# Three small moves in a four-layer fp32 backbone: the reciprocal root, differential attention's reciprocals, and the Nyquist copies

## The chip, the cores and the metric

The kernel runs on one core of a Trainium2 chip. The core has a matrix engine (TensorE; PE in the profile, and PEld for its weight loads), VectorE (DVE), ScalarE (ACT), GpSimd (POOL), SyncE (SP) and DMA queues. Each engine takes its own instructions in its own order, and engines wait for one another through semaphores. The metric is the device time of one launch in microseconds (us), less being better; a comparison uses the median of several launches. Durations of single instructions come from one profiled launch.

## What is computed

A backbone over 512 latent and 256 context tokens of width 1024, four layers deep. Layer i mixes tokens by kind i mod 3 (Fourier, differential attention, latent attention, Fourier again) and then runs a squared-ReLU MLP. Every sub-layer begins with an RMS norm, so a reciprocal root of a mean square stands at the head of each; differential attention has one more norm per head on its output. Cut to what the change touches:

```python
def rms_norm(x, g, eps=RMS_EPS):
    y = x * lax.rsqrt(jnp.mean(x * x, axis=-1, keepdims=True) + eps)
    return y * g

def diff_attend(q1, q2, k1, k2, v, lam):          # 8 heads, two maps each
    p = jax.nn.softmax(s1, axis=-1) - lam * jax.nn.softmax(s2, axis=-1)
    return jnp.einsum("bhqk,bkhe->bqhe", p, v)    # then rms_norm over the head

def fourier_mixer(h, w, bias):                    # layers 0 and 3
    f = jnp.fft.fft2(h_grouped, axes=(1, 3), norm="ortho").real
    return f.reshape(b, s, d) @ w + bias
```

## The kernel before

Activations lie transposed, features on the 128 partitions: `x` is eight tiles of 128 x 768 (512 latent, 256 context columns). Every fp32 matrix product is made of three TensorE products: each operand is split into a high part (a cast on ScalarE, L96) and a low part (a subtraction on VectorE, L97), and high*high, high*low and low*high are summed. So weights, activations and probabilities all pass once through ScalarE and once through VectorE before TensorE can use them. VectorE also adds each layer's result to `x` (`accum`, L375), which is what empties the PSUM buffers that TensorE fills (`pw`, `pu`, `ps` in the rows).

TensorE's program is in the order in which the code is written. The instructions of the other engines are put in order by a scheduler, from priorities and its own cost estimates, so that an edit can move instructions that it does not name. What each place of the change does:

- **`rstd_from`** (L283 to L289) makes `r = 1/sqrt(ms/n + eps)` from a sum of squares `ms` in PSUM: logarithm (L284) and exponential (L286) on ScalarE give a first value, then one Newton step sharpens it: a square on ScalarE (L287), and on VectorE `v` from `ms` (L285), a product (L288) and a fused multiply-add (L289). It is called by the norm that ends an MLP and feeds the next layer (`MixNorm.finish`, L309), by the norm that feeds an MLP (`MlpNorm.stat`, L359), by the head norm of differential attention (`PVb`, L992), by latent attention's two inner norms (`lat_norm`, L1123) and at the start for six columns of one element per partition (L627).
- **`S`** in `diff` (L933 to L959) computes two score maps for a block of 128 query tokens. For each map VectorE takes the row maximum (L952), ScalarE the exponential with its row sum (L953), VectorE the reciprocal of the sum (L954). The second reciprocal is multiplied by lambda on VectorE (L956), ScalarE scales map 2 with it (L957) and VectorE scales map 1 and subtracts (L958). There are 32 such blocks of 768 keys and 16 of 256 keys (context), hence 48 pairs of maps. `Tr` transposes the result on TensorE (L801), `PVa` multiplies by the values, `PVb` normalises. Between these steps TensorE is given work of other heads (`F(...)`): projections, and for the odd heads the output projection `gen_wo`, whose results go to `x` by L375 with two `pw` buffers.
- **`fourier_lat`** (L752, layer 3) transforms along the group's features first: for each of 4 groups and 4 token tiles one product of 258 columns in `pw` (three buffers), split into `fa` (high on ScalarE, low on VectorE, both read `pw`). Column 256, the Nyquist term, is copied from both parts into small tiles `nqh` and `nql` by GpSimd (L777, L778), 32 copies of 128 x 1; a product over the four token tiles (L785) reads them. The first eight products use the first 256 tokens; after the fourth, `flush()` (L781) runs the rest of the previous norm for tokens 256 to 511: a product `ms`, `rstd_from`, and then for each of 8 feature tiles `nu` (VectorE, L328), `hhi` (ScalarE, L329) and `hlo` (VectorE, L330), which the second eight products need. `csl` (L97) are low parts of the table for the second transform.

## Time and profile before

| | |
|---|---|
| time of three launches | 2876.17, 2877.42 (median), 2878.32 us |
| the profiled launch itself | 2874.33 us, of which 2872.5 us are the profile's span |
| mean granted TensorE clock | 0.984 of full |
| instructions | 39661 |
| DMA | 294.00 MB, mean 102 GB/s |

How to read a row of the profile: in a timeline, start and length in us, engine, line, operation, output <- inputs, shapes, count, and in brackets how long the engine sat idle just before and on which instruction it then stopped waiting. In a table of windows: the stretch and its length, busy time (and count) of PE, PEld, DVE, ACT and POOL, the granted TensorE clock as a share of full, the share of DMA time, and GB/s. In the table of waits: the engine and its instruction <- what it waited for, total us, times, longest. In a table by form: line, engine, operation, names, shapes and count | busy us, mean ns | idle time before, with what ended it.

### The profile page before, as it was taken

The numbers are of one execution on the slowest core, as the hardware profiler recorded it, in microseconds if no ns is written. First come the engines' busy times: TensorE is split into PE (matmuls) and PEld (weight loads), VectorE is DVE, ScalarE is ACT, GpSimd is POOL, SyncE is SP. The second block draws the span as 40 slices with busy tenths as digits, with TensorE's granted clock in tenths as the row PEclk, the third lists the DMA queues.
The fourth block names the chain that finished last, engine by engine and source line by source line (L and its number), as shares of the span: only waits on it lengthen the run. The fifth ranks groups of instructions, "written<-read, shape, count | busy, mean of one in ns | idle before, by whom it ended". The sixth has DMA issues, their size and how long they took to land.

```text
span 2872.5 us, 39661 instructions
## 1 busy us (share of the span) xinstructions
PE 2737.2 (95%) x15387; PEld 2357.4 (82%) x15387; DVE 1924.1 (67%) x3371; ACT 1265.6 (44%) x2301; POOL 314.5 (11%) x267
## 2 busy tenths in 40 slices
PE   8999999999999899799999998899899998999998
PEld 5788888888888778688888897788778888888887
DVE  8986665658787778775545448998875546564344
ACT  4542222225575656432323236777543335443332
POOL 0010000002110010100000012665200003100001
PEclk9999999999999999999999999999999998999999
DMA  9454333322111111253333311110455542233231
GB/s 323 149 183 131 111 110 110 110 96 90 44 46 46 40 45 41 96 161 117 112 116 117 96 38 50 33 46 19 149 189 182 165 136 67 92 96 100 77 116 46
DMA packets 95452, 294.00 MB, mean 102 GB/s; under 512 B 11264, under 2 KB 15520, under 8 KB 94752
## 3 DMA queue, kind: packets, MB, share of 16 engines
q1 hardware_dynamic: 92704, 288.33, 31.8%
q0 software_dynamic: 2560, 3.15, 0.6%
q8 instruction: 121, 1.98, 0.3%
q14 instruction: 67, 0.55, 0.1%
HBM read 283.29 MB, written 2.11 MB: 99 GB/s over the span
## 4 chain that ended last, share of the span: by engine, by line
PE 78%; DVE 14%; ACT 4%; DMA 2%; issue 2%; POOL 0%; SPq 0%; POOLq 0%; ACTq 0%; DVEq 0%
PE pw L140 70%; PE pu L140 4%; PE ps L140 3%; DVE ptl L97 2%; DVE x L375 1%; DVE mx L952 1%; PE pu L801 1%; ACT e L1292 1%; DVE mx L1290 1%; DVE wlo L97 1%; DVE nu L328 1%; DVE hlo L330 1%; PE pn L140 1%; DVE hlo L348 0%; DMA raw<-in_w 0%
## 5 line engine op out<-in xcount | busy, mean ns | idle before, releaser
L96 ACT CAST whi<-raw 128x1024 fp32r<-128x1024 f32 (+1 forms) x322 | 308.4, 984 | 1081.4 <-PE pw L140 1018.0
L140 PE MATMUL pw<-hhi,whi 128*128 128x512 f32 (+2 forms) x1680 | 590.3, 351 | 4.1 <-DVE r L450 3.2
L140 PE MATMUL pw<-hlo,whi 128*128 128x512 f32 (+2 forms) x1680 | 589.5, 351 | 0.0
L140 PE MATMUL pw<-hhi,wlo 128*128 128x512 f32 (+2 forms) x1680 | 587.6, 350 | 0.8 <-DVE wlo L97 0.8
L140 PE MATMUL pw<-ahi,whi 128*128 128x512 f32 (+1 forms) x1664 | 568.9, 342 | 1.2 <-ACT ahi L96 1.2
L140 PE MATMUL pw<-alo,whi 128*128 128x512 f32 (+1 forms) x1664 | 567.5, 341 | 1.1 <-DVE alo L97 1.1
L140 PE MATMUL pw<-ahi,wlo 128*128 128x512 f32 (+1 forms) x1664 | 566.3, 340 | 0.0
L375 DVE SCALAR_TENSOR_TENSOR x<-pw,mod,x 128x512 f32<-128x512 f32 (+1 forms) x504 | 302.0, 623 | 286.0 <-PE pw L140 283.2
L97 DVE TENSOR_TENSOR wlo<-raw,whi 128x1024 fp32r<-128x1024 f32 (+1 forms) x322 | 362.5, 1142 | 169.7 <-ACT whi L96 168.4
L140 PEld LDWEIGHTS pw<-hhi,whi 128*128 128x128 f32 x1680 | 318.5, 190 | 48.6 <-issue 3.4
L140 PEld LDWEIGHTS pw<-hhi,wlo 128*128 128x128 f32 x1680 | 318.9, 190 | 44.1 <-DVE wlo L97 1.3
L140 PEld LDWEIGHTS pw<-hlo,whi 128*128 128x128 f32 x1680 | 318.5, 190 | 42.5
L140 PEld LDWEIGHTS pw<-ahi,whi 128*128 128x128 f32 x1664 | 315.6, 190 | 38.5 <-ACT ahi L96 1.7
L140 PEld LDWEIGHTS pw<-alo,whi 128*128 128x128 f32 x1664 | 315.5, 190 | 37.0 <-DVE alo L97 1.6
L140 PEld LDWEIGHTS pw<-ahi,wlo 128*128 128x128 f32 x1664 | 315.2, 189 | 36.2
L264 DVE SCALAR_TENSOR_TENSOR raw<-raw,cb 128x1024 f32<-128x1024 f32 x176 | 214.9, 1222 | 118.6 <-DMA raw<-in_modw 116.9
L307 POOL TENSOR_TENSOR nacc<-nacc,nsq 128x256 f32<-128x256 f32 x70 | 53.2, 760 | 1752.1 <-ACT nsq L306 1751.2
L264 DVE SCALAR_TENSOR_TENSOR junk<-raw,cb 128x1024 bf16<-128x1024 f32 x96 | 118.8, 1238 | 66.4 <-DMA raw<-in_modw 64.6
L1294 POOL TENSOR_SCALAR e<-e,li 128x768 f32<-128x768 f32 x64 | 145.5, 2279 | 93.3 <-DVE li L1293 70.9
L97 DVE TENSOR_TENSOR alo<-r,ahi 128x768 fp32r<-128x768 f32 (+2 forms) x134 | 105.7, 792 | 73.5 <-ACT ahi L96 73.2
L97 DVE TENSOR_TENSOR ptl<-pu,pth 128x384 fp32r<-128x384 f32 (+1 forms) x208 | 106.1, 539 | 8.4 <-ACT pth L96 5.6
L140 PE MATMUL pw<-hhi,g 128*128 128x512 f32 (+2 forms) x384 | 100.9, 344 | 5.0 <-DVE x L375 2.9
(330 smaller groups left out, 4287.1 us busy)
## 6 DMA issues: line engine op xcount, KB each, us to landing
raw<-in_w SPq DMA_DIRECT2D x252, 512.0 KB, 4.0
raw<-in_modw SPq DMA_DIRECT2D x176, 512.0 KB, 3.8
wm<-in_msh SPq DMA_DIRECT2D x32, 256.0 KB, 5.9
raw<-in_fw SPq DMA_DIRECT2D x10, 512.0 KB, 4.0
cb<-scr SPq DMA_DIRECT2D x4, 1024.0 KB, 5.5
raw<-in_dwk SPq DMA_DIRECT2D x16, 256.0 KB, 2.7
raw<-in_dwq SPq DMA_DIRECT2D x16, 256.0 KB, 2.8
raw<-in_dwv SPq DMA_DIRECT2D x16, 256.0 KB, 2.6
```

The lines of the kernel that those rows point to most:

```text
L96: nc.scalar.copy(hi, src)
L97: nc.vector.tensor_sub(lo, src, rd(hi))
L140: r = nc.tensor.matmul(o, lhsT, rhs, start=start, stop=stop)
L264: nc.vector.scalar_tensor_tensor(o, m, 1.0, cb[:, v * 1024:(v + 1) * 1024], op0=ALU.mult, op1=ALU.mult, accum_out=mcol(mod[l, ch], v, k))
L307: nc.gpsimd.tensor_tensor(nacc[:, c0:c0 + w], nacc[:, c0:c0 + w], s, op=ALU.add)
L328: nc.vector.scalar_tensor_tensor(u, xs, am, r, op0=ALU.mult, op1=ALU.mult)
L330: nc.vector.scalar_tensor_tensor(lo, u, sh, rd(hi), op0=ALU.add, op1=ALU.subtract)
L375: nc.vector.scalar_tensor_tensor(xs, src, mcol(mod[l, ch], 0 if c0 < SL else 1, n), xs, op0=ALU.mult, op1=ALU.add)
L801: nc.tensor.transpose(t[:, i * 128:(i + 1) * 128], p[:, (k0 + i) * 128:(k0 + i + 1) * 128], ident)
L952: nc.vector.reduce_max(mx, sv, axis=AX.X, negate=True)
L1290: nc.vector.reduce_max(mx, s[:, :T], axis=AX.X, negate=True)
L1294: nc.gpsimd.tensor_scalar(et, et, li, None, op0=ALU.mult)
```

## The change

`rstd_from` loses one VectorE operation and its scratch tile `v`. The factor one half and 1/n go into the scale of ScalarE's square, and the sum of squares is added to eps*n and multiplied in one VectorE operation that reads PSUM; the last one computes (1.5 - t)*r. In differential attention both row sums go to the two columns of one tile, one reciprocal of 128 x 2 serves both maps, and lambda is applied by a 128 x 1 operation on ScalarE. In layer 3 the Nyquist copies are made by ScalarE in place of GpSimd.

```diff
-    def rstd_from(ms, inv_n, r, t, v):
+    def rstd_from(ms, inv_n, r, t):
         nc.scalar.activation(t, ms, AF.Ln, bias=epst[0:t.shape[0]], scale=inv_n)
-        nc.vector.tensor_scalar(v, ms, -0.5 * inv_n, -0.5 * EPS, op0=ALU.mult, op1=ALU.add)
         nc.scalar.activation(r, t, AF.Exp, scale=-0.5)
-        nc.scalar.activation(t, r, AF.Square)
-        nc.vector.tensor_mul(t, t, v)
-        nc.vector.scalar_tensor_tensor(r, t, 1.5, r, op0=ALU.add, op1=ALU.mult)
+        nc.scalar.activation(t, r, AF.Square, scale=math.sqrt(0.5 * inv_n))
+        nc.vector.scalar_tensor_tensor(t, ms, EPS / inv_n, t, op0=ALU.add, op1=ALU.mult)
+        nc.vector.scalar_tensor_tensor(r, t, 1.5, r, op0=ALU.subtract, op1=ALU.mult, reverse0=True)
...
-                        nc.gpsimd.tensor_copy(nq[t][0][:, 32 * g:32 * g + 1], rd(ah[:, 256:257]))
-                        nc.gpsimd.tensor_copy(nq[t][1][:, 32 * g:32 * g + 1], rd(al[:, 256:257]))
+                        nc.scalar.copy(nq[t][0][:, 32 * g:32 * g + 1], rd(ah[:, 256:257]))
+                        nc.scalar.copy(nq[t][1][:, 32 * g:32 * g + 1], rd(al[:, 256:257]))
...
                 for _, _, o0, w_, e in rows:
-                    ri = []
+                    li = sp.tile([128, 2], F32, name="li", tag="li", bufs=4)
                     for m in range(2):
                         mx = sp.tile([128, 1], F32, name="mx", tag="mx", bufs=4)
-                        li = sp.tile([128, 1], F32, name="li", tag="li", bufs=4)
                         sv = s[m][:, o0:o0 + w_]
                         nc.vector.reduce_max(mx, sv, axis=AX.X, negate=True)
-                        nc.scalar.activation(e[m], sv, AF.Exp, bias=mx, accum_out=li)
-                        nc.vector.reciprocal(li, li)
-                        ri.append(li)
-                    nc.vector.tensor_mul(ri[1], ri[1], lam)
-                    nc.scalar.activation(e[1], e[1], AF.Copy, scale=ri[1])
-                    nc.vector.scalar_tensor_tensor(e[0], e[0], ri[0], e[1], op0=ALU.mult, op1=ALU.subtract)
+                        nc.scalar.activation(e[m], sv, AF.Exp, bias=mx, accum_out=li[:, m:m + 1])
+                    nc.vector.reciprocal(li, li)
+                    nc.scalar.activation(li[:, 1:2], li[:, 1:2], AF.Copy, scale=lam)
+                    nc.scalar.activation(e[1], e[1], AF.Copy, scale=li[:, 1:2])
+                    nc.vector.scalar_tensor_tensor(e[0], e[0], li[:, 0:1], e[1], op0=ALU.mult, op1=ALU.subtract)
```

The callers drop their last argument. The order of TensorE and SyncE is the same in both programs; the scheduler moves instructions on VectorE and ScalarE; three places are shown. Line numbers behind `rstd_from`'s first lines are smaller in the changed program (its L287 and L288 are the two VectorE operations, L776 and L777 the copies, L535 is L536 of before).

VectorE in layer 3 around the flushed norm, before: the fourth low part (`fa_22701`), table parts, the norm's chain, then the fifth low part (`fa_22780`).

```order
L97 TENSOR_TENSOR csl1_22758<-raw_22755,csh1_22757 128x516
L288 TENSOR_TENSOR nt_22709<-nt_22709,nv_22710 128x256
L97 TENSOR_TENSOR csl2_22764<-raw_22761,csh2_22763 128x516
L289 SCALAR_TENSOR_TENSOR nr_22708<-nt_22709,nr_22708 128x256
L97 TENSOR_TENSOR csl3_22770<-raw_22767,csh3_22769 128x516
L328 SCALAR_TENSOR_TENSOR nu_22717<-x0_70,am3_1_119,nr_22708 128x256
L328 SCALAR_TENSOR_TENSOR nu_22721<-x1_71,am3_1_119,nr_22708 128x256
L97 TENSOR_TENSOR fa_22780<-pw_22773,fa_22780 128x258
```

The same place of VectorE in the changed program; `fa_22592`, `fa_22604` and `fa_22616` are the fifth, sixth and seventh low part.

```order
L97 TENSOR_TENSOR csl3_22582<-raw_22579,csh3_22581 128x516
L287 SCALAR_TENSOR_TENSOR nt_22523<-pn_22520,nt_22523 128x256
L97 TENSOR_TENSOR fa_22592<-pw_22585,fa_22592 128x258
L288 SCALAR_TENSOR_TENSOR nr_22522<-nt_22523,nr_22522 128x256
L97 TENSOR_TENSOR fa_22604<-pw_22597,fa_22604 128x258
L327 SCALAR_TENSOR_TENSOR nu_22529<-x0_70,am3_1_119,nr_22522 128x256
L327 SCALAR_TENSOR_TENSOR nu_22533<-x1_71,am3_1_119,nr_22522 128x256
L97 TENSOR_TENSOR fa_22616<-pw_22609,fa_22616 128x258
```

All table parts now stand ahead of the chain, and the fifth and sixth low parts have moved from behind `nu` to between the chain's steps.

ScalarE at the end of the first transform in layer 3, in the changed program: the last two casts, the last four copies, a weight cast `g` and the biases added to `x` (before, the same casts and biases stand there without copies).

```order
L96 CAST fa<-pw 128x258 x2
L776 CAST nqh_22464<-fa 128x1
L96 CAST g<-raw 128x512
L776 CAST nqh_22468<-fa 128x1
L535 ACTIVATE x_70<-x_70,gb 128x512
L777 CAST nql_22465<-fa 128x1
L535 ACTIVATE x_71<-x_71,gb 128x512
L777 CAST nql_22469<-fa 128x1
```

The last copy stands behind one weight cast and two bias operations.

VectorE in differential attention at a head's first output projection, before: head norm, row maxima, the additions to `x`.

```order
L285 TENSOR_SCALAR nv<-pu 128x256
L288 TENSOR_TENSOR nt<-nt,nv 128x256
L289 SCALAR_TENSOR_TENSOR nr<-nt,nr 128x256
L997 SCALAR_TENSOR_TENSOR nu<-nu,gs,nr 128x256
L952 TENSOR_REDUCE mx<-ps 128x1
L375 SCALAR_TENSOR_TENSOR x_71<-pw,mod_2_104,x_71 128x512
L97 TENSOR_TENSOR ol<-nu,oh 128x256
L952 TENSOR_REDUCE mx<-ps 128x1
```

The same place in the changed program (its L994, L950 and L374 are L997, L952 and L375 of before).

```order
L287 SCALAR_TENSOR_TENSOR nt<-pu,nt 128x256
L288 SCALAR_TENSOR_TENSOR nr<-nt,nr 128x256
L994 SCALAR_TENSOR_TENSOR nu<-nu,gs,nr 128x256
L97 TENSOR_TENSOR ol<-nu,oh 128x256
L950 TENSOR_REDUCE mx<-ps 128x1
L374 SCALAR_TENSOR_TENSOR x_71<-pw,mod_2_104,x_71 128x512
L950 TENSOR_REDUCE mx<-ps 128x1
```

`v` is gone, and `ol`, which waits for ScalarE's cast `oh` of `nu`, has moved ahead of the first row maximum and of the first addition to `x`.

More of the change, by code (lines that the diff above doesn't have):

```diff
@@ L314, in finish @@
             r = nt_("r")
-            rstd_from(ms, 1.0 / D, r, nt_("t"), nt_("v"))
+            rstd_from(ms, 1.0 / D, r, nt_("t"))
             v = 0 if c0 < SL else 1
@@ L366, in stat @@
             for c0, ms in zip(range(0, self.T, 256), ps):
-                rstd_from(ms, 1.0 / D, r_all[:, c0:c0 + 256], nt_("t"), nt_("v"))
+                rstd_from(ms, 1.0 / D, r_all[:, c0:c0 + 256], nt_("t"))
     def parts(T):
@@ L626, in fourier_first @@
                     nc.scalar.activation(jk, xr, AF.Square, accum_out=ss[:, 0:1])
-                rstd_from(ss[:, 0:1], 1.0 / D, ss[:, 1:2], ss[:, 2:3], ss[:, 3:4])
+                rstd_from(ss[:, 0:1], 1.0 / D, ss[:, 1:2], ss[:, 2:3])
                 uh = up.tile([128, 1024], F32R, name="uh")
@@ L995, in PVb @@
                 r = nt_("r")
-                rstd_from(ms, 1.0 / 128, r, nt_("t"), nt_("v"))
+                rstd_from(ms, 1.0 / 128, r, nt_("t"))
                 nc.vector.scalar_tensor_tensor(u, u, gs, r, op0=ALU.mult, op1=ALU.mult)
@@ L1127, in lat_norm @@
                 r = qt_("r")[:, :w]
-                rstd_from(ms, inv_n, r, qt_("t")[:, :w], qt_("v")[:, :w])
+                rstd_from(ms, inv_n, r, qt_("t")[:, :w])
                 for i, p in enumerate(ps):
```

## The prediction

> **What bounds the kernel now.** I read the page's busy shares, then the windows, to find the stages in which TensorE waits, and there its waits.
>
> ```profile
> PE 2737.2 (95%) x15387; PEld 2357.4 (82%) x15387; DVE 1924.1 (67%) x3371; ACT 1265.6 (44%) x2301; POOL 314.5 (11%) x267
> core 0: us, PE busy (x) PEld busy (x) DVE busy (x) ACT busy (x) POOL busy (x), PEclk, DMA share, GB/s
> 200.00:250.00 50.00, 50.00 (x289) 44.02 (x288) 37.68 (x59) 15.65 (x20) 0.00 (x0) 1.00 0.44 135
> 760.00:1150.00 390.00, 355.84 (x2290) 315.24 (x2289) 313.11 (x666) 242.94 (x546) 30.66 (x37) 0.99 0.16 42
> 2408.00:2441.00 33.00, 25.43 (x134) 22.51 (x133) 27.10 (x61) 22.28 (x52) 15.75 (x45) 0.74 0.22 67
> ```
>
> TensorE is busy 95% of the span, and in an MLP (200 to 250) without a gap: a reciprocal root that is a little sooner there buys nothing. It is idle 390 - 356 = 34 us in differential attention (760 to 1150), where VectorE is 80% busy, and 7.6 us at the start of layer 3 (2408 to 2441), where its clock is only 0.74 besides. The change touches the work that stands in the way in both. In attention half of that idle time ends on one VectorE operation, the addition to `x` (the table of TensorE's waits):
>
> ```profile
> PE pw L140 <- DVE x L375: 16.7, 16, 2.2
> ```
>
> **Differential attention, step by step.** The operations that go, by form between 700 and 1200, and a pair of rows that shows what a small one really takes:
>
> ```profile
> L954 DVE RECIPROCAL li<-li 128x1 f32<-128x1 f32 x96 | 14.6, 156 | 7.1 <-ACT e L953 4.7 <-ACT nacc L953 1.7
> L285 DVE TENSOR_SCALAR nv<-pu 128x256 f32<-128x256 f32 x25 | 10.5, 421 | 15.7 <-ACT nt L284 15.5
> L956 DVE TENSOR_TENSOR li<-li,lam 128x1 f32<-128x1 f32 x48 | 7.3, 152 | 0.5
> 993.59 0.15 DVE L956 TENSOR_TENSOR li<-li,lam 128x1 f32<-128x1 f32 x1
> 993.66 0.68 DVE L874 TENSOR_TENSOR qt<-qt,qsw 128x512 f32<-128x512 f32 x1
> ```
>
> 48 reciprocals and 48 products go, and 25 computations of `v`. By busy time that is 7.3 + 7.3 + 10.5 = 25.1 us. But a small operation lets the next one start 0.07 us after itself, so the 96 small ones may free only 6.7 us, and 25 of `v` at 0.42 free 10.5: 17 us at the low end, 25 at the high end, of 313 us. I take 17, for the next operation's start is what counts on a busy VectorE.
>
> Little of it will reach TensorE. Of the 15.7 us that VectorE stood before `v`, none is won by its going: the product behind it waits for ScalarE's square, two operations later, and its successor waits there in the same way. The rows at one output projection show the rest:
>
> ```profile
> 998.99 0.42 DVE L285 TENSOR_SCALAR nv<-pu 128x256 f32<-128x256 f32 x1
> 999.51 0.42 DVE L288 TENSOR_TENSOR nt<-nt,nv 128x256 f32<-128x256 f32 x1
> 1002.79 0.42 DVE L97 TENSOR_TENSOR ol<-nu,oh 128x256 fp32r<-128x256 f32 x1
> 1004.92 0.47 DVE L375 SCALAR_TENSOR_TENSOR x<-pw,mod,x 128x256 f32<-128x256 f32 x1
> 1005.45 0.39 PE L140 MATMUL pw<-oh,whi 128*128 128x256 f32 x1 [1.99 <-DVE x L375]
> ```
>
> Without `v` the chain is 999.51 - 998.99 = 0.5 us earlier, but `ol` now stands ahead of the first addition and takes 0.42 of it back; the addition at 1004.92, for which TensorE waits 1.99, comes 0.1 to 0.5 us sooner. The 16 such waits at 0.1 to 0.25 give 2 to 4 us; **I take -3**. The ends: -17, if every freed microsecond were one of TensorE's, and +4, for what ScalarE gets to do. That is 48 operations of 128 x 1 with a pointer as scale, which before does not show; the nearest row (shortest, median and longest ns) is 128 x 1 at the kernel's start, with a pointer as bias:
>
> ```profile
> L284 ACT ACTIVATE ss<-ss,epst x6: 279/285/296, 7.6 to 22.0; 128x1 f32<-128x1 f32 x6
> ```
>
> 48 x 0.285 = 13.7 us. ScalarE was 62% busy (242.9 of 390) and VectorE's product that it replaces stood in the same chain, so I charge nothing; the cover is that idle 38%, and if it failed at, say, three in ten of the operations, it would be the +4.
>
> **Layer 3.** Here is the largest single wait that the change touches:
>
> ```profile
> 2419.79 0.38 ACT L96 CAST fa<-pw 128x258 fp32r<-128x258 f32 x1 [0.58 <-PE pw L140]
> 2420.06 0.42 ACT L287 ACTIVATE nt<-nr 128x256 f32<-128x256 f32 x1
> 2420.51 0.42 DVE L288 TENSOR_TENSOR nt<-nt,nv 128x256 f32<-128x256 f32 x1 [1.31 <-ACT nt L287]
> 2422.91 0.91 ACT L329 ACTIVATE hhi<-nu,mod 128x256 fp32r<-128x256 f32 x2 [2.03 <-DVE nu L328]
> 2423.19 0.42 DVE L97 TENSOR_TENSOR fa<-pw,fa 128x258 fp32r<-128x258 f32 x1
> 2423.53 0.87 DVE L330 SCALAR_TENSOR_TENSOR hlo<-nu,mod,hhi 128x256 fp32r<-128x256 f32 x2
> 2424.32 0.87 DVE L328 SCALAR_TENSOR_TENSOR nu<-x,am,nr 128x256 f32<-128x256 f32 x2
> 2423.66 0.80 PE L140 MATMUL pw<-g,hhi 128*128 128x258 f32 x2 [3.19 <-DVE fa L97]
> 2425.67 0.77 PE L140 MATMUL pw<-g,hhi 128*128 128x258 f32 x2 [0.35 <-DVE fa L97]
> ```
>
> The eighth product waits 3.19 us for a buffer whose low part, the fifth, could have been taken at 2419, but stands behind the whole chain and `nu`. In the changed order one cast fewer stands between logarithm and square, so the square comes about 0.5 us sooner (it waited behind the cast at 2419.79), and the fifth low part stands right behind the first VectorE step: 2419.7 + 0.42 + 0.42 = 2420.5 in place of 2423.6. The eighth product starts there, 3.1 us sooner. The ninth, the first that needs the new half, waits for `hhi`: `nu` starts behind the second step and one more low part, 2420.5 + 0.42 + 0.42 = 2421.4, `hhi`, which before began at 2422.91, behind two casts and four copies at 2421.8, the product at about 2422.2 in place of 2425.67, **3.5 us sooner**. What follows hangs on the clock:
>
> ```profile
> 2419.60:2423.00 3.40, 0.88 (x7) 0.67 (x6) 2.49 (x6) 1.15 (x4) 0.82 (x2) 1.00 0.42 108
> 2423.00:2426.40 3.40, 2.39 (x9) 2.12 (x10) 2.75 (x8) 1.86 (x5) 0.67 (x3) 0.50 0.72 283
> 2433.20:2436.60 3.40, 3.40 (x18) 3.40 (x17) 2.65 (x4) 1.81 (x6) 2.16 (x3) 0.50 0.29 88
> 1180.70:1184.10 3.40, 1.67 (x10) 1.00 (x8) 3.40 (x5) 0.73 (x1) 2.57 (x2) 1.00 0.03 5
> 1190.90:1194.30 3.40, 1.51 (x8) 1.25 (x9) 3.40 (x7) 2.59 (x6) 0.77 (x1) 0.99 0.02 7
> 1194.30:1197.70 3.40, 3.40 (x9) 2.64 (x8) 1.82 (x2) 0.59 (x1) 3.32 (x2) 0.51 0.73 301
> ```
>
> After a stretch of 3.4 us in which TensorE worked 0.88 the clock is halved in the next, and still in the last of four (2433.2); after 1.51 (1190.9) it is halved too, after 1.67 (1180.7) not. With the gap gone, the stretch from 2419.6 holds some 2.1 us of work, so full speed may last longer. Then VectorE sets the pace, by the starts at 2423.19, 2423.53 and 2424.32: two `hlo` or two `nu` take 0.79, a low part 0.34, so a pair of products takes 2 x 0.79 + 2 x 0.34 = 2.3 us and four pairs 9.2, in place of 2437.8 - 2425.7 = 12.1 (from the ninth product to the Nyquist product, below): another 2.9 sooner. At half clock it stays 12.1. A later gap probably halves it anyway; I count 0.7 of the 2.9.
>
> The copies:
>
> ```profile
> L96 ACT CAST hhi<-mod 128x2 fp32r<-128x2 f32 x8 | 1.2, 184 | 0.0
> 2438.06 0.63 ACT L96 CAST g<-raw 128x512 fp32r<-128x512 f32 x1
> 2437.77 0.28 PE L140 MATMUL pn<-csh,nqh 128*128 128x258 f32 x1
> 2440.45 0.39 PE L140 MATMUL pn<-csh,nql 128*128 128x258 f32 x1 [0.43 <-POOL nql L778]
> 2439.36 3.18 ACT L536 ACTIVATE x<-x,gb 128x512 f32<-128x512 f32 x5
> ```
>
> A copy of one column costs about 0.18 on ScalarE (the 128 x 2 cast, the nearest row), 32 of them 5.9 us, of which most lies in ScalarE's 33 - 22.3 = 10.7 idle us. The last ones do not: behind the last cast stand four copies, a weight cast (0.63) and two biases (3.18 for five), 0.7 + 0.6 + 1.3 = 2.6 us and some 0.2 for the cast itself to begin, 2.8, against the 2440.45 - 2437.77 = 2.7 that GpSimd takes now: +0.1. Layer 3 in sum: -3.5 - 0.7 + 0.1, **about -4**; the ends are -3.5 - 2.9 = -6.4 and, with all 5.9 us of copies on the path, -3.5 + 5.9 = +2.4.
>
> The Trainium skill ("TensorE: Matmul & The Clock Gate", Part 1) says that the clock is halved after an idle window of 3.4 us and restored after a busy one, in windows that do not start with the kernel. The length agrees with the rows above, the condition does not: 1.51 us of work in the window did not save the clock. By the page alone no gap here would halve it, and layer 3 would give -3.5 - 2.9 + 0.1 = -6.3 in place of -4, which is rival (b) below.
>
> **The end of attention.** `ms` now is read until the square is there, so its buffer comes free later:
>
> ```profile
> 1156.30 0.42 DVE L285 TENSOR_SCALAR nv<-pu 128x256 f32<-128x256 f32 x1 [1.02 <-ACT nt L284]
> 1156.78 0.90 PE L801 MATMUL pu<-ident,e 128*128 128x128 f32 x3 [0.39 <-DVE nv L285]
> 1156.98 0.42 ACT L287 ACTIVATE nt<-nr 128x256 f32<-128x256 f32 x1
> ```
>
> The second transpose of the last block takes that buffer. It would start behind 1156.98 + 0.42 + 0.42 = 1157.8, less 0.3 for a cast that no longer stands before the square, in place of 1156.78: **+0.8**. Elsewhere TensorE has other work between, and it costs nothing. The start and the other norms change by less than the rows resolve.
>
> **Sum**: -3 - 4 + 0.8 = -6.2. The profiled launch took 2874.3, which gives 2868.1; the median of the launches lies 3.1 higher, so I expect **2871**, with 2865 to 2877 for this case.
>
> **Rivals.** (a) VectorE is the bound of attention in earnest, and all 17 us come back: 2877.4 - 17 - 4 + 0.8 = 2857, or 2863 if two thirds do. For it speaks that half of the idle time ends on one of VectorE's operations; against it, that few removed operations stand right ahead of one. (b) The clock in layer 3 stays up to the Nyquist product: 2871 - 2.2 = 2869; the rows leave it open, since 1.51 us of work let the clock fall and 1.67 did not. (c) The change removes operations but no time: VectorE waits as long for ScalarE's square and exponentials, and the scheduler puts something else ahead: 2877.4 + 0.8 = 2878. (d) Slower: ScalarE becomes late in layer 3. Its copies of the low part wait for VectorE in ScalarE's own order, and casts and `hhi` queue behind. With 5.9 us on the path, the 3.5 lost again because the fifth cast comes late, and two more stretches of 3.4 us at half clock (1.7 each), layer 3 gives +9.3, the kernel 2877.4 + 9.3 + 0.8 = 2887. It decides where TensorE's work in a stretch of 3.4 us falls below about 1.6.
>
> **Chances.** Forecast 0.42, (a) 0.12, (b) 0.13, (c) 0.2, (d) 0.13. A measurement of this kernel can tell about 0.2% (5.8 us) from no change: faster than 2871.7 are (a), (b) and half of the forecast, 0.46; within, the other half and (c), 0.41; slower (d), 0.13. The range 2859 to 2882 leaves out (d) and the far part of (a).
>
> **What would show it.** Right: VectorE between 760 and 1150 some 17 us less busy while TensorE's idle time there falls by 2 to 4; no wait above 1.5 us for `fa` in layer 3; a wait of about 2 us before the last Nyquist products, now on ScalarE; a longer wait of one transpose at 1157. Wrong: TensorE's waits for `x` unchanged or longer (c); waits for `fa` or `hhi` that end on ScalarE (d); a drop of more than 8 us in attention (a).

## The result, and the profile after

The changed kernel takes **2858.57 us** (median of six launches, 2855.88 to 2863.02) against 2876.80 for the kernel before on the same chip: a ratio of **0.9948, 95% interval 0.9936 to 0.9959**, some 15 us. In a second set of launches it took 2860.64 against 2875.48, again 0.9948 (0.9936 to 0.9961). (The medians lie 18 us apart, a little more than the ratio says; gains below go by the ratio.) The forecast, 2871, had the sign right and was less than half the gain. The median lies 0.4 us under the low end of the range; as a ratio, 0.9948 of the 2877.4 from which the forecast started, it is 2862, inside. The starting point was itself a little high: the larger sets of launches of before that follow have medians of 2874.7 to 2875.5.

The busy times of the profile's page, and three stretches of the table of windows (columns as before: stretch and length, busy us and count of PE, PEld, DVE, ACT, POOL, granted clock, DMA share, GB/s), of the profiled launch of after, the longest of its six (2863.02 us, span 2861.2). The second stretch begins and ends with the same matmuls as 745 to 1141 before, whose row follows:

```profile
PE 2733.4 (96%) x15387; PEld 2354.1 (82%) x15387; DVE 1898.6 (66%) x3222; ACT 1276.9 (45%) x2381; POOL 304.0 (11%) x235
...
760.00:1150.00 390.00, 356.58 (x2301) 316.17 (x2299) 301.19 (x563) 254.21 (x600) 30.02 (x37) 0.99 0.16 45
744.50:1135.60 391.10, 361.11 (x2347) 321.59 (x2346) 301.23 (x561) 254.62 (x598) 31.04 (x39) 0.99 0.17 46
...
2408.00:2441.00 33.00, 26.70 (x181) 24.10 (x181) 28.17 (x65) 28.70 (x91) 4.74 (x10) 0.95 0.31 96
```

Before:

```profile
745.00:1141.00 396.00, 362.59 (x2347) 322.11 (x2346) 317.37 (x674) 247.36 (x552) 31.68 (x39) 0.99 0.17 45
```

Between the same matmuls VectorE is 16 us less busy in attention (317.4 to 301.2), and TensorE's idle time falls from 33.4 us to 30.0. The fixed stretch of 760 to 1150 hides that: it shows 12 us and 33.4 after 34.2, since after does 11 matmuls more in it. At the start of layer 3 the clock is up from 0.74 to 0.95.

**Where the time went.** TensorE's program is the same in every kernel of this study, so the time between the same two matmuls can be compared exactly, stage by stage. The columns are the stretches that begin and end with the matmuls that before starts at these times; all in us.

| one profiled launch of | MLP of layer 0 begins (184 to 215) | attention (745 to 1141) | its end (1141 to 1217) | MLP of layer 2 begins (2050 to 2110) | layer 3 begins (2420 to 2470) |
|---|---|---|---|---|---|
| before | 30.9 | 396.0 | 76.0 | 59.9 | 49.9 |
| after | 27.8 | 391.1 | 80.4 | 57.5 | 43.8 |
| after, second launch (`e9_again`) | 27.5 | 391.6 | 79.9 | 59.1 | 44.0 |
| `e1_root` | 28.1 | 391.7 | 75.7 | 57.7 | 43.4 |
| `e2_attn` | 31.0 | 392.9 | 75.2 | 60.3 | 49.5 |
| `e3_copies` | 30.7 | 394.6 | 79.5 | 60.1 | 45.3 |
| `e4_order` | 30.9 | 393.5 | 75.3 | 59.3 | 45.4 |
| `e5_mlp` | 26.6 | 394.6 | 79.6 | 59.3 | 49.9 |
| `e6_mix` | 31.0 | 395.6 | 75.2 | 58.8 | 44.7 |
| `e7_step` | 32.4 | 391.2 | 75.7 | 60.4 | 43.9 |
| `e8_headnorm` | 32.2 | 390.4 | 76.4 | 60.0 | 47.6 |
| `e10_rootcopies` | 26.1 | 389.7 | 81.2 | 58.6 | 45.2 |
| `e11_tables` | 26.3 | 390.7 | 80.5 | 58.4 | 45.1 |
| `e12_lamdve` | 31.5 | 392.8 | 81.3 | 59.8 | 47.2 |

Rows without an edit in a stage show what launches differ by there: 1.5 us at the start of layer 0's MLP, 2.5 in attention, 4.4 at its end, 1.5 at layer 2's MLP, 2.7 in layer 3 (47.2 to 49.9). The first surprise is in the first column: 3 us gone at the start of an MLP, where the prediction had seen no gap. The second is that the end of attention, 4 us longer in after, is as long in two kernels without an edit there, `e3_copies` and `e5_mlp`.

Most of what launches differ by is the clock. For the same stretches, the time in which TensorE ran no matmul, and the time at half clock, lowest to highest of each group of launches, in us:

| stretch | launches | TensorE idle | at half clock |
|---|---|---|---|
| MLP of layer 0 | 7 without the new root there | 3.1 to 3.8 | 3.4 to 6.8 |
| | 6 with it (`e7_step`: 3.6 and 6.8) | 0.0 to 1.6 | 0 |
| attention | 5 without an edit there | 33.3 to 33.6 | 3.4 to 10.2 |
| | `e2_attn`, `e12_lamdve` | 32.3, 33.2 | 6.8, 3.4 |
| | 7 with the new root | 29.8 to 30.7 | 6.8 to 10.2 |
| its end | 7 that took 75.2 to 76.4 us | 15.1 to 17.4 | 13.7 to 17.1 |
| | 7 that took 79.5 to 81.3 us | 15.7 to 16.7 | 23.9 to 34.1 |
| MLP of layer 2 | 7 without the new root there | 1.9 to 3.4 | 4.2 to 6.8 |
| | 6 with it (`e7_step`: 2.7 and 7.6) | 1.5 to 2.1 | 4.2 to 7.4 |
| layer 3 | 5 without an edit there | 7.4 to 8.5 | 6.8 to 17.1 |
| | 9 with one | 5.1 to 6.3 | 3.4 to 10.2 |

So the two values at the end of attention are more or fewer stretches at half clock, with the same idle time.

### The profile page after: what moved, and what is told of

Read it like the earlier page. It is cut to its first block, busy times and chain, and to the rows that moved or that the text cites. A ratio compares the mean times of both kernels' runs of the same rounds, so it can differ in the third digit from the quotient of the medians.

```text
span 2861.2 us, 39526 instructions
## 1 busy us (share of the span) xinstructions
PE 2733.4 (96%) x15387; PEld 2354.1 (82%) x15387; DVE 1898.6 (66%) x3222; ACT 1276.9 (45%) x2381; POOL 304.0 (11%) x235
## 4 chain that ended last, share of the span: by engine, by line
PE 77%; DVE 14%; ACT 5%; DMA 2%; issue 2%; POOL 0%; POOLq 0%; SPq 0%; ACTq 0%; DVEq 0%
PE pw L140 69%; PE pu L140 4%; PE ps L140 2%; DVE x L374 1%; DVE ptl L97 1%; PE pu L800 1%; DVE wlo L97 1%; DVE mx L950 1%; ACT e L1289 1%; DVE hlo L329 1%; DVE nu L327 1%; DVE mx L1287 1%; ACT pth L96 1%; DVE junk L264 0%; DVE raw L264 0%
## 5 line engine op out<-in xcount | busy, mean ns | idle before, releaser
L374 DVE SCALAR_TENSOR_TENSOR x<-pw,mod,x 128x512 f32<-128x512 f32 (+1 forms) x504 | 302.2, 623 | 283.0 <-PE pw L140 281.9
L140 PEld LDWEIGHTS pw<-hhi,whi 128*128 128x128 f32 x1680 | 318.3, 189 | 45.3 <-DVE qt L871 1.4
L97 DVE TENSOR_TENSOR ptl<-pu,pth 128x384 fp32r<-128x384 f32 (+1 forms) x208 | 106.6, 540 | 13.8 <-ACT pth L96 10.7
```

What stands on the lines that cost most here:

```text
L97: nc.vector.tensor_sub(lo, src, rd(hi))
L140: r = nc.tensor.matmul(o, lhsT, rhs, start=start, stop=stop)
L374: nc.vector.scalar_tensor_tensor(xs, src, mcol(mod[l, ch], 0 if c0 < SL else 1, n), xs, op0=ALU.mult, op1=ALU.add)
```

## The experiments

All against before on the same chip; a minus is faster. The us are the ratio less one, times 2875.

| kernel | what it is | median, us | ratio (95% interval) | us |
|---|---|---|---|---|
| `e1_root` | reciprocal root alone | 2859.25 | 0.9940 (0.9927 to 0.9953) | -17.2 |
| `e2_attn` | attention's part alone | 2875.53 | 0.9998 (0.9987 to 1.0009) | -0.6 |
| `e3_copies` | Nyquist copies alone | 2869.38 | 0.9978 (0.9968 to 0.9988) | -6.3 |
| `e4_order` | nothing removed, order of layer 3 only | 2870.04 | 0.9980 (0.9970 to 0.9989) | -5.8 |
| `e5_mlp` | root, only ahead of the MLPs | 2870.00 | 0.9982 (0.9970 to 0.9993) | -5.2 |
| `e6_mix` | root, only behind the MLPs | 2870.63 | 0.9980 (0.9971 to 0.9990) | -5.8 |
| `e7_step` | `e1_root` and an empty step in the MLPs' roots | 2866.67 | 0.9967 (0.9955 to 0.9980) | -9.5 |
| `e8_headnorm` | root, only in attention's head norm | 2869.08 | 0.9978 (0.9969 to 0.9987) | -6.3 |
| `e9_again` | the changed kernel | 2860.64 | 0.9948 (0.9936 to 0.9961) | -15.0 |
| `e10_rootcopies` | the change without attention's part | 2856.63 | 0.9939 (0.9925 to 0.9952) | -17.5 |
| `e11_tables` | the change, tables of layer 3 later | 2857.19 | 0.9945 (0.9933 to 0.9958) | -15.8 |
| `e12_lamdve` | one reciprocal, lambda on VectorE | 2872.57 | 0.9992 (0.9983 to 1.0001) | -2.3 |

### Each part alone

**`e1_root`**: before, with the new `rstd_from` at all its callers (the first hunk of the change), and nothing else.

> The reciprocal root alone (one VectorE operation less in each), the rest as before. Theory 'order': what layer 3 gained is the place of the fifth low part on VectorE. Here it stands behind the whole chain but ahead of the two nu, not between the chain's steps, so about half of the 7.6 us that layer 3 gained between the two traces: -2 to -4 there; attention -0.5 to -1.5 (v's place); in sum -3 to -6 by the medians. Rival 'operations': the shorter chain itself is the gain, so layer 3 gives all of -6 to -8 here and the kernel -7 to -9. Rival 'clock': what differs is where gaps fall in the 3.4 us windows of the clock; then pieces of 1.7 and 3.4 us appear in stages that the edit does not touch (layer 0's MLP at 194, layer 2's MLP at 2060), and the launches of one kernel spread by 5 us or more.

-17.2 us: the root alone gives all that the whole change gives. Layer 3 gave 6.5 and attention 4.3 in the trace, but there are also 2.8 and 2.2 us at the two MLP starts, which the expectation had called untouched and left to the rival "clock". In layer 3 the expectation's "half" was too little: at 43.4 us it stands with the whole change, and 6.5 us is what the rival "operations" had named there (6 to 8). `e3_copies` and `e4_order` tell the two apart.

**`e2_attn`**: before, with the change's hunk in `S`: one reciprocal of 128 x 2, lambda on ScalarE.

> Differential attention's part alone (one reciprocal for both maps, lambda on ScalarE), roots and copies as before. Theory 'order and little VectorE': attention -1.5 to -3.5, layer 3 within 0.5 of before, end of attention within 1 of before (the root still reads its sum of squares early, so a buffer is not held); kernel -2 to -4. Rival 'VectorE bounds attention': the 96 operations removed less 48 give back 5 us or more there. Rival 'clock': pieces of 1.7 and 3.4 us elsewhere.

-0.6 (-3.7 to +2.6): nothing that launches can tell, where -2 to -4 was expected. The trace has 392.9 us in attention, 2.0 less than the mean of the five rows without an edit there (394.9), but only 1.1 less idle time. The rival, 5 us or more, falls.

**`e3_copies`**: before, with the copies of column 256 made by `nc.scalar.copy`.

> The Nyquist copies on ScalarE alone. Theory 'order': VectorE's order in layer 3 changes here too (the fifth low part moves from behind two nu to just behind the chain), so layer 3 gives -1.5 to -4 although not one VectorE operation goes; TensorE's wait for the fifth low part falls from 3.2 us to some 2; attention unchanged; kernel -1.5 to -4. Rival 'operations': 0 to +1, the wait of 3.2 us stays and the last copies come a little later. Rival 'clock': pieces of 1.7 and 3.4 us elsewhere.

-6.3 us, though no operation goes and ScalarE gets 32 more. The waits of TensorE between 2400 and 2470 (what waited <- what it waited for: total us, times, longest), `e3_copies`:

```profile
PE pw L140 <- DVE fa L97: 5.2, 6, 2.1
...
PE pn L140 <- ACT nqh L777: 0.7, 1, 0.7
```

The wait of 3.19 us for the fifth low part is down to 2.1, as expected from its new place behind the chain and ahead of the two `nu`; the Nyquist product now waits 0.7 for a copy. Rival "operations" falls. The stage is 45.3 us, 3.5 less than the mean of the five rows without an edit in layer 3 (48.8); the kernel's -6.3 (-9.2 to -3.5) is more than was expected, and no other stretch of the table shows the rest.

**`e4_order`**: nothing removed, nothing moved between engines; the split of the first transform's result gets a higher priority.

```diff
-                        split(ah, al, p[:, 0:258])
+                        with tc.high_priority(200):
+                            split(ah, al, p[:, 0:258])
```

> Before, with the split of the first transform's result in layer 3 at a raised priority and nothing removed: on VectorE the fifth, sixth and seventh low part now stand ahead of the norm's chain, the table parts behind. Theory 'order': the wait of 3.2 us for the fifth low part goes without one operation less; layer 3 gives -4 to -8, the kernel the same. Rival 'operations': without a shorter chain the new half's first product is as late as before (2425.7), and layer 3 gives 0 to -1.5. Rival 'clock': pieces of 1.7 and 3.4 us elsewhere.

-5.8 us, and layer 3 45.4 us, like the copies. The same table of waits, `e4_order`:

```profile
PE pw L140 <- ACT hhi L329: 4.0, 3, 2.8
...
PE pw L140 <- DVE fa L97: 0.8, 1, 0.8
```

The waits for `fa` have all but gone (5.7 us before), and a wait of 2.8 us for the new half, `hhi`, has come, since the low parts now stand in the way of the norm's chain. The rival "operations" had the new half's first product as late as before; it starts 6.4 us behind the norm's matmul, where the five launches without an edit have 8.1 to 9.6 and the six with the new root there 5.9 to 6.0. With no operation removed TensorE's idle time is 6.0 us, within the 5.1 to 6.3 of the nine launches with an edit. So what is won in layer 3 is a matter of order on VectorE, and three different edits reach it. Whether the 1.2 us between this kernel and the mean with the new root (44.2) is the shorter chain cannot be told: launches differ by 2.7 there.

### The root, place by place

**`e5_mlp`**, **`e6_mix`**, **`e8_headnorm`**: before, with the new root at one kind of caller: `MlpNorm.stat`, `MixNorm.finish`, `PVb`.

> The shorter root only in the norm that feeds an MLP (the sums of squares of all tokens, twelve roots in the kernel in all four layers), all else as before. Theory 'slots': at the start of layer 0's MLP VectorE gets three 1.2 us products of the modulation fewer between the steps of three roots, so TensorE's wait for r (3.23 us at 193.6) falls to about 0.5 and the half clock behind it goes: -3 there; layer 2's MLP -2 (waits for hlo, ahi and wlo of 1.2 us and less go); layer 3's Fourier part unchanged within 0.5; kernel -4 to -6. Rival 'launches': the gains at 194 and 2084 belong to the launches profiled and come and go; the median within 1.5 of before.

> The shorter root only in the norm between an MLP and the next layer's mixer (and the last norm), all else as before. Theory 'order': layer 3's Fourier part -4 to -6.5 as with all roots shorter, the two MLP starts (194, 2084) unchanged; kernel -5 to -8. With the MLP norm alone this should make up most of the 15 us that all roots give. Rival: the gain of layer 3 comes from elsewhere (the end of layer 2's MLP, or the clock), and it stays under 2.

> The shorter root only in differential attention's norm of each head, all else as before. The trace of the root alone is 4.3 us shorter between 745 and 1141, but two kernels without any edit there were 1.4 and 2.5 shorter too. Theory 'little': attention -1 to -2 and the kernel -1 to -2; by the prediction's working (16 additions to x each 0.1 to 0.25 sooner) -1.6 to -4. Rival 'VectorE bounds attention': 25 operations of 0.42 come back, -8 or more. End of attention: by the prediction +0.8 since a buffer is held; the trace of after has +4.3 there, of the copies alone +3.5 with no edit there, so it should be within what launches differ by, -1 to +4.

(The roots ahead of the MLPs are ten, not twelve: three in each of layers 0 and 1, two in each of 2 and 3.) -5.2, -5.8 and -6.3, each to within 3 us: in sum -17.3, the root's -17.2. The root's gain has three places of about equal size, and each trace shows it in its own stage: the start of layer 0's MLP 26.6 where kernels without that edit have 30.7 to 32.2; layer 3 44.7 where kernels without an edit there have 47.2 to 49.9; attention 390.4 where they have 393.5 to 396.0. For `e8_headnorm` the expectation, 1 to 2 us, was too little, and the ratio gave more than the trace's 4.5 us in attention; its end of attention, 76.4 us, shows no longer stay. At the start of layer 2's MLP `e5_mlp` has 59.3 us, no gain that one trace can show.

### Why the start of an MLP gained

VectorE's timeline before, at the third of the three roots that feed layer 0's MLP (start, length, engine, line, operation, output <- inputs; `raw`, `junk` and `wlo` have nothing to do with the norm), and the matmul that waits for `r`:

```profile
188.05 0.42 DVE L285 TENSOR_SCALAR nv<-pn 128x256 f32<-128x256 f32 x1 [0.28 <-ACT nt L284]
188.39 1.22 DVE L264 SCALAR_TENSOR_TENSOR raw<-raw,cb 128x1024 f32<-128x1024 f32 x1
...
189.53 0.42 DVE L288 TENSOR_TENSOR nt<-nt,nv 128x256 f32<-128x256 f32 x1
189.87 1.22 DVE L97 TENSOR_TENSOR wlo<-raw,whi 128x1024 fp32r<-128x1024 f32 x1
191.00 0.41 DVE L289 SCALAR_TENSOR_TENSOR rall<-nt,rall 128x256 f32<-128x256 f32 x1
191.34 1.22 DVE L264 SCALAR_TENSOR_TENSOR junk<-raw,cb 128x1024 bf16<-128x1024 f32 x1
...
192.48 1.81 DVE L450 TENSOR_TENSOR r<-pw,rall 128x768 f32<-128x768 f32 x2
193.58 0.47 PE L140 MATMUL pw<-hhi,whi 128*128 128x512 f32 x1 [3.23 <-DVE r L450]
```

The same place in `e1_root`:

```profile
187.06 0.42 DVE L287 SCALAR_TENSOR_TENSOR nt<-pn,nt 128x256 f32<-128x256 f32 x1
187.40 0.15 DVE L445 COPY bt<-pw 128x2 f32<-128x2 f32 x1
187.51 0.43 DVE L288 SCALAR_TENSOR_TENSOR rall<-nt,rall 128x256 f32<-128x256 f32 x1
187.86 1.22 DVE L264 SCALAR_TENSOR_TENSOR junk<-raw,cb 128x1024 bf16<-128x1024 f32 x1
...
189.00 1.82 DVE L449 TENSOR_TENSOR r<-pw,rall 128x768 f32<-128x768 f32 x2
190.10 0.47 PE L140 MATMUL pw<-hhi,whi 128*128 128x512 f32 x1 [0.53 <-DVE r L449]
```

Before, behind each of the root's three steps stands one operation of 1.22 us: a product of the modulation or a weight's low part. VectorE takes its instructions in order, so `r` waits for these as well. From the first step of the first root to `r` before has ten of them in 14.9 us (177.60 to 192.48), `e1_root` seven in 11.1 (177.87 to 189.00). One step less in each of three roots took 3 x 0.34 us of its own and three such slots of 1.14 with it (both by the starts of what stands behind), 4.4 us, of which a longer wait for a weight's cast took some back: 3.8 are left. (In the third root of `e1_root` the small copy `bt` holds one such place.) TensorE waited 3.23 us for `r` and now 0.53.

Behind the wait of before stands a stretch at half clock (granted clock 0.50):

```profile
194.11:197.52 3.41, 3.41 (x10) 2.63 (x9) 3.11 (x7) 3.41 (x7) 0.00 (x0) 0.50 0.41 127
```

All eight traces with three steps in these roots have one or two such stretches of 3.41 us, the first beginning between 192 and 195, and the six with two steps have none. At half the clock 3.41 us do the work of 1.7. That, and 2.6 us less idle time on average, make up about the 4 us that the stage gained.

**`e7_step`** takes the root alone and puts a step without work between the two that are left, only ahead of the MLPs:

```diff
+        nc.vector.tensor_copy(t[:, 0:1], t[:, 0:1])
```

> All roots shorter, as in the root alone, but in the norm that feeds an MLP a copy of one column onto itself (128 x 1) stands between the two VectorE steps. It costs VectorE about 0.07 to 0.15 us each, 36 columns' worth in nothing; but it is a third step, and the scheduler puts a 1.2 us modulation product behind it, three more ahead of r in layer 0's MLP. Theory 'slots': TensorE's wait for r is back at about 3 us and so are the 3 us at 194; kernel +3 to +6 against the root alone (-15), so -9 to -12 against before. Rival 'busy time': what helped is 0.42 us of VectorE's work less for each root; then three steps of 0.1 give back 0.3 us at most and the kernel stays at -14 to -16.

-9.5 (-12.9 to -5.8) where the root alone has -17.2 (-21 to -13.5): 7.7 lost to a copy of one column, where 3 to 6 was expected. In the two traces the MLP starts differ by 4.3 and 2.7. Its timeline at the same place:

```profile
189.27 0.42 DVE L294 SCALAR_TENSOR_TENSOR nt<-pn,nt 128x256 f32<-128x256 f32 x1
189.62 1.22 DVE L264 SCALAR_TENSOR_TENSOR raw<-raw,cb 128x1024 f32<-128x1024 f32 x1
...
190.76 0.15 DVE L295 COPY nt<-nt 128x1 f32<-128x1 f32 x1
190.82 1.22 DVE L264 SCALAR_TENSOR_TENSOR junk<-raw,cb 128x1024 bf16<-128x1024 f32 x1
...
191.96 0.42 DVE L296 SCALAR_TENSOR_TENSOR rall<-nt,rall 128x256 f32<-128x256 f32 x1
...
193.44 1.82 DVE L457 TENSOR_TENSOR r<-pw,rall 128x768 f32<-128x768 f32 x2
194.54 0.76 PE L140 MATMUL pw<-hhi,whi 128*128 128x512 f32 x1 [3.62 <-DVE r L457]
```

The copy itself holds VectorE 0.06 us (190.76 to 190.82), yet there are eleven operations of 1.22 between the first step and `r` again, and the wait is back at 3.62. What counted was the number of steps, not their work. Layer 2's MLP lost its gain too (60.4 us); there TensorE's waits between 2050 and 2110 were, before and in `e1_root` (both have 0.6 for `alo` besides):

```profile
PE pw L140 <- DVE hlo L348: 1.4, 2, 0.8
PE pw L140 <- ACT ahi L96: 1.2, 1, 1.2
PE pw L140 <- DVE wlo L97: 0.8, 2, 0.5
```

```profile
PE pw L140 <- DVE wlo L97: 0.3, 1, 0.3
```

How the steps shifted the order there was not followed row by row.

### The change again, and three variants

**`e9_again`** is the changed kernel, unchanged.

> The changed kernel once more, for a second trace on this chip and as the mark for the three beside it. By the parts measured alone (the root's three places give -5.0, -4.3 and -5.9, in sum -15; all roots together -15.4; attention's part -0; copies -5, in the same place as the root's layer 3) it should be 14 to 18 under before. Theory 'launches' for the end of attention (+4.3 in its first trace at 1141 to 1217): a second launch lies anywhere between 75 and 80 us there, as launches without an edit there do. Rival 'held buffer': again about 80, 4 more than before.

-15.0; the stages repeat. The end of attention is 79.9 us again, which is what the rival said. But `e3_copies` and `e5_mlp`, with no edit there, have 79.5 and 79.6, and `e1_root` and `e8_headnorm`, which hold the buffer too, 75.7 and 76.4: the stage takes two values, by how much of it runs at half clock, and the edit does not decide which.

**`e10_rootcopies`** leaves attention's part out of the change.

> The changed kernel without attention's part (two reciprocals and the product with lambda on VectorE, as before). Theory 'attention's part is worth little': within 2 of the changed kernel; between 745 and 1141 390 to 392, like the root alone, where the changed kernel has 391. Rival 'the reciprocals matter': 3 to 5 slower than the changed kernel.

-17.5, not slower than the whole change but 2.5 us faster, where 2 either way was expected; 389.7 us in attention, 30.4 of them idle where the whole change has 30.0 and 30.1. Attention's part brings nothing beside the root that shows. The two intervals overlap, so it cannot be called a better kernel either.

**`e11_tables`** is the change with the table parts of layer 3 loaded behind the twelfth product of the first transform in place of the fourth:

```diff
                     if tt[0] == 0 and g == 1:
                         flush()
+                    if tt[0] == 2 and g == 1:
                         cs = [load_table(tp, "cs", t, 516) for t in range(4)]
```

> The changed kernel with layer 3's table parts loaded two groups later in the program: on VectorE only two of the four low parts of the tables (0.6 us each) stand ahead of the norm's chain and the fifth low part. Theory 'order': the fifth low part and the new half come some 1.2 us sooner, layer 3 gives -1 to -2 more, if the last two table parts are not late for the Nyquist product; kernel -1 to -2 against the changed one, which medians can just not tell and the trace can. Rival: the two table parts now stand ahead of the Nyquist product and give the time back, 0 to +2.

-15.8, and 45.1 us in layer 3 against 43.8 and 44.0: counted from the norm's matmul the eighth product comes 1.4 us sooner than in after and the ninth 0.8, but the longest wait for `hhi` is 1.6 us where it was 0.9, and nothing is left at the end of the stage: 5.5 us of idle time where after has 5.8, and 6.8 us at half clock where it has 3.4.

**`e12_lamdve`** is attention's part with lambda still on VectorE:

```diff
-                    nc.scalar.activation(li[:, 1:2], li[:, 1:2], AF.Copy, scale=lam)
+                    nc.vector.tensor_mul(li[:, 1:2], li[:, 1:2], lam)
```

> Before, with one reciprocal of two columns for both maps, but lambda still multiplied on VectorE (128 x 1, 48 times), so that ScalarE gets no operation. Theory 'ScalarE pays nothing': like attention's part with lambda on ScalarE, 392 to 394 between 745 and 1141 (before: 393.5 to 396 in five launches without an edit there). Rival 'ScalarE pays': the 48 operations of 0.30 on ScalarE cost what VectorE's freed ones bring; then this is 2 to 4 faster than attention's part alone, 389 to 391 there.

-2.3 (-4.9 to +0.3), 392.8 us in attention against 392.9 with lambda on ScalarE: the 48 small operations on ScalarE cost nothing that TensorE shows, and the rival "ScalarE pays" (389 to 391) falls.

## Why the prediction was right and wrong, step by step

**"... and in an MLP (200 to 250) without a gap: a reciprocal root that is a little sooner there buys nothing."** This is the step that failed. The stretch was taken behind the place where the root works: the wait of 3.23 us for `r` ends at 193.58, as long as the one in layer 3 that was called the largest. Kernels with the new root ahead of the MLPs have 27.1 us on average in 184 to 215 and 58.4 in 2050 to 2110, those without it 31.2 and 59.7 (`e7_step`, with its extra step, counted with neither): **4.1 + 1.3 = 5.4 us that the sum did not hold**. `e5_mlp` alone gives -5.2, and `e7_step` gives it back. The step put the MLPs at nothing; the wait for `r` fell from 3.23 to 0.53 and the half clock behind it went.

**Attention, -3 with ends of -17 and +4: right in size, and in part in its source.** The forecast freed 17 us of VectorE and gave TensorE 2 to 4, through the shorter chain of the head norm's root. VectorE is 16 us less busy between the same matmuls and TensorE's idle time is down by 3.4. With the new root the stage has 390.8 us on average of four traces and 391.1 of three with attention's part as well, against 394.9 without an edit: -4.1 and -3.8. The head norm's root gives all of it, as the forecast had it. Alone it makes VectorE 8 us less busy and TensorE 3 less idle. The 48 reciprocals and 48 products, 96 of the 121 operations freed here, free as much of VectorE (8 us in `e2_attn`), take 1.1 us off the idle time alone (the reciprocals without the products, `e12_lamdve`, 0.2) and next to nothing on top of the root. Equal time freed on VectorE is worth 3 us in one place and one or none in the other, so the gain goes with the chain and not with VectorE's load. The operations by form between 700 and 1200, after, show what took their place (line, engine, operation, shapes and count | busy us, mean ns | idle before):

```profile
L953 ACT ACTIVATE li<-li,lam 128x1 f32<-128x1 f32 x48 | 14.4, 300 | 5.6 <-DVE li L952 5.5
...
L287 DVE SCALAR_TENSOR_TENSOR nt<-pu,nt 128x256 f32<-128x256 f32 x25 | 10.5, 422 | 29.1 <-ACT nt L286 28.8
...
L952 DVE RECIPROCAL li<-li 128x2 f32<-128x2 f32 x48 | 7.7, 161 | 9.7 <-ACT e L951 5.9 <-ACT nacc L951 3.4
```

A reciprocal of two columns costs what one of one column did (161 ns against 156), and lambda on ScalarE 300 ns where 285 was taken. VectorE's new idle time stands ahead of the root's first step: 29.1 us, where `v` and the product had 15.7 and 4.5. Much of the time freed became a longer wait for ScalarE's square, as the prediction said of `v`'s 15.7. The total of the waits for `x`:

```profile
PE pw L140 <- DVE x L374: 14.6, 15, 1.9
```

It was 16.7 in 16: 2.1 us, the low end of the 2 to 4 that the forecast saw in these waits. With the root alone they fall by only 0.6 (16.0 to 15.4 between the same matmuls, also in `e8_headnorm`), and the rest of its 3 us lies in smaller waits, for `wlo` above all (3.0 to 0.9). So the size came out, but less of it at the place named. Rival (a), all 17 us, and (c), no time, both fall.

**Layer 3, -4: right.** The norm's matmul before, then TensorE's rows and VectorE's chain after; times are counted from the norm's matmul (2416.06 before, 2413.66 after):

```profile
2416.06 1.13 PE L140 MATMUL pn<-nacc,ones 128*128 128x256 f32 x2 [0.24 <-POOL nacc L307]
```

```profile
2413.66 0.70 PE L140 MATMUL pn<-nacc,ones 128*128 128x256 f32 x2 [0.26 <-POOL nacc L306]
2417.70 0.50 PE L140 MATMUL pw<-g,hhi 128*128 128x258 f32 x2 [1.17 <-DVE fa L97]
2419.56 0.80 PE L140 MATMUL pw<-g,hhi 128*128 128x258 f32 x2 [0.87 <-ACT hhi L328]
...
2429.71 0.28 PE L140 MATMUL pn<-csh,nqh 128*128 128x258 f32 x1
...
2431.74 0.39 PE L140 MATMUL pn<-csh,nql 128*128 128x258 f32 x1 [0.80 <-ACT nql L777]
...
2432.44 0.39 PE L140 MATMUL pn<-csh,nql 128*128 128x258 f32 x1
```

```profile
2416.90 0.41 DVE L287 SCALAR_TENSOR_TENSOR nt<-pn,nt 128x256 f32<-128x256 f32 x1
2417.24 0.41 DVE L97 TENSOR_TENSOR fa<-pw,fa 128x258 fp32r<-128x258 f32 x1
2417.57 0.41 DVE L288 SCALAR_TENSOR_TENSOR nr<-nt,nr 128x256 f32<-128x256 f32 x1
```

The fifth low part stands where the order put it, the wait for it is 1.17 in place of 3.19. From the norm's matmul the eighth product starts (2423.66 - 2416.06) - (2417.70 - 2413.66) = 3.6 us sooner (forecast 3.1), the ninth (2425.67 - 2416.06) - (2419.56 - 2413.66) = 3.7 (forecast 3.5). Before's launch flatters both: three of the five launches without an edit have the ninth at 8.1 us behind the norm's matmul, where this one has 9.6 and after 5.9, so the edit alone is worth 2.2 to 3.7. To the Nyquist product it is (2437.77 - 2425.67) - (2429.71 - 2419.56) = 1.95 more, where 0.7 of at most 2.9 was counted: the clock was halved once here, not four times. From the first to the last Nyquist product it is 2432.44 - 2429.71 = 2.73 us where GpSimd took 2.68, the forecast +0.1; but the longest wait for a copy, 0.80 us on ScalarE, is far from the 2 us that was named as its sign. Over launches the stage has 44.2 us with the new root or the change (six traces), 48.8 without an edit: -4.6 for the forecast -4, some 2 us of it idle time and the rest less half clock. Rival (d), ScalarE late, falls: the new waits for `hhi` (1.3 us in three, the longest 0.9) and for a copy stayed small.

Rival (b), the clock up until the Nyquist product, did not come. The Trainium skill ("TensorE: Matmul & The Clock Gate", Part 1) gives an idle window of some 3.4 us as what brings the half clock, but tells in the same part of a kernel whose short idle times between matmuls brought it too, which the prediction's "no gap here would halve it" left out. The trace sides with the latter; in after, three stretches of the table of windows:

```profile
2416.30:2419.70 3.40, 1.36 (x10) 0.95 (x8) 3.30 (x10) 2.37 (x11) 0.00 (x0) 0.97 0.94 299
2419.70:2423.10 3.40, 3.40 (x15) 3.14 (x15) 2.88 (x8) 2.76 (x11) 0.00 (x0) 0.53 0.42 151
2423.10:2426.50 3.40, 2.71 (x17) 2.10 (x16) 3.23 (x9) 2.81 (x13) 0.00 (x0) 1.00 0.00 0
```

TensorE worked 1.36 of 3.40 us and its longest wait was 1.17, and the clock was halved all the same, for one window. So the gain lay between the forecast's case and (b).

**The end of attention, +0.8: the size came by luck, and the stage's time does not show it.** The second transpose of the last block waits 1.16 us after, and comes 1.54 us after the matmul ahead of it where before it came 0.80 after; VectorE's rows beside it:

```profile
1151.24 0.90 PE L800 MATMUL pu<-ident,e 128*128 128x128 f32 x3 [1.16 <-DVE ptl L97]
```

```profile
1150.62 0.56 DVE L97 TENSOR_TENSOR ptl<-pu,pth 128x384 fp32r<-128x384 f32 x1 [2.14 <-ACT pth L96]
1151.39 0.42 DVE L287 SCALAR_TENSOR_TENSOR nt<-pu,nt 128x256 f32<-128x256 f32 x1 [0.21 <-ACT nt L286]
```

That is +0.74, close to the forecast, and all seven launches with the new root here have 1.5 to 1.8 us where the seven others have 0.8. But the mechanism is not the forecast's: the transpose starts at 1151.24, before VectorE has read the held sum of squares (L287, 1151.39 to 1151.81), so it cannot have waited for that buffer. It waited for the one that `ptl` reads, until 1151.18. Why it takes another buffer than before was not tried. The stage as a whole is 75 to 76 or 79 to 81 us with the edit and without it, by the clock, so the term cannot be read from the time.

**The sum.** Forecast: -3 - 4 + 0.8 = -6.2. By the stages: -3.8 - 4.6 - 5.4 = -13.8 (the end of attention left out), of the -15 measured. Of the 8.8 us between forecast and ratio 5.4 are the MLP starts, attention and layer 3 a little larger than forecast and the end of attention left out make 2.2, and 1.2 no stage of the traces shows. The other 3.6 of the 12.4 us between 2871 and 2858.57 lie between the median and the ratio: 15 us under the forecast's start is 2862.

## What to carry to other kernels

Where a scheduler fills the gaps of a dependent chain on an in-order engine, a chain costs its steps, not their work: each step can let one more unrelated operation in ahead of the result (here 1.14 us each), and an edit that removes a step is to be priced by what stands behind it. Look for the place where an operation's result is first needed in every stage that uses it, with windows that begin ahead of that place. An engine that is 80% busy can lose a hundred small operations and give nothing that launches can tell, if its waits only grow by the same. And compare stages between the same two instructions, with idle time and half clock apart: the idle time of a stage without an edit repeated to 0.3 us in attention, where its length differed by 2.5.

## What the hardware showed unasked

**The clock's windows lie on a grid of 3.41 us that starts at another phase in each launch, and the half clock costs what falls into it.** In all fourteen traces the changes of the clock lie whole multiples of 3.41 us apart; the first line of that grid lies 2.97 us behind the span's start in before, 2.85 in after and 0.34 in `e9_again`. With nearly the same program TensorE's clock was halved for 75 to 103 us in all. The same short gaps near 2457, in a stage that no edit touched, halved one window in before (1.57 us of work in the window ahead) and in `e9_again` (1.88 of work), and none in the first launch of after; before's two windows, then those of `e9_again`:

```profile
2457.20:2460.60 3.40, 1.57 (x7) 0.89 (x6) 1.81 (x5) 1.07 (x3) 0.00 (x0) 0.99 0.22 77
2460.60:2464.00 3.40, 3.40 (x10) 2.64 (x9) 2.11 (x4) 1.65 (x4) 0.00 (x0) 0.50 0.22 77
```

```profile
2447.50:2450.90 3.40, 1.88 (x7) 1.03 (x6) 2.32 (x5) 0.99 (x2) 0.00 (x0) 1.00 0.23 77
2450.90:2454.30 3.40, 3.40 (x10) 2.61 (x9) 2.17 (x4) 1.94 (x4) 0.00 (x0) 0.53 0.14 39
```

Counted over all fourteen traces from the starts and lengths of the matmuls, from 90 us on, each full-clock window with under 1.5 us of work was followed by half clock (92 of 92), none with over 2.2 was, and between these it went both ways (92 of 258 fell); full speed came back only behind a window with at least 2.75 us of work, and not behind each of those (184 of 214). A single trace therefore carries differences in a stage (4.4 us at the end of attention) that owe nothing to the edit, and it takes several launches of kernels that share the stage to read a gain of that size.
